# Weight sums of the gated half on the vector engine, and the place of the casts of loaded sums, in a gMLP layer

## The chip, the cores and the metric

The kernel runs on one core of a Trainium2 chip. Its engines work side by side, each through its own queue in order: TensorE (PE in the profile; PEld is its weight load), VectorE (DVE), ScalarE (ACT), GpSimd (POOL) and SyncE (SP), which here only issues DMAs. The metric is the device time of one execution in microseconds (us); lower is better. Runs of before lie between 1413.17 and 1414.5 us.

## What is computed

Two layers of a residual trunk over 512 tokens of width 1024, all in float32. Each has a token mixer and a squared-ReLU MLP, both normed and modulated. Layer 0 mixes with chunked attention; layer 1 with a spatial gating, which is where the change lies:

```python
def chunked_spatial_gating(h, w_in, v_gain, w_s, b_s, w_out):
    z = jax.nn.gelu(h @ w_in, approximate=False)          # 512 x 6144
    u, v = jnp.split(z, 2, axis=-1)
    v = rms_norm(v, v_gain).reshape(B, nw, SG_WINDOW, SG_GROUPS, SG_HALF // SG_GROUPS)
...
    vm = jnp.einsum('gij,bnjgc->bnigc', w, v) + b_s.T...
    return (u * vm.reshape(B, S, SG_HALF)) @ w_out
```

`v`, the gated half, needs its norm over all 3072 columns before the first product with `u` can be made, so the kernel computes all of `v` first.

## The kernel before

**Products.** A float32 product is made of three passes: each operand is split into a high part, a cast to fp32r by ScalarE, and a low part, the rest, by VectorE (class `Split`, lines 485 and 486), and `mm3` runs high by high, high by low and low by high (line 92).

**Seven instead of eight.** A product of 512 x 1024 activations with a 1024 x 1024 piece of a weight is cut into 2 x 2 blocks and made with seven block products in place of eight (`seven`, line 611), a Strassen-like scheme. The seven right operands are sums of the weight's blocks: (0,0); (1,0); (0,0)+(0,1); (1,1); (0,0)+(0,1)+(1,1); (0,1)+(1,1); and the sum of all four. They are taken in the order m = 0, 1, 2, 4, 3, 5, 6. Each is handled in two halves (s = 0, 1), so a product is 14 steps of 12 matmuls. Block (0,0) is loaded as `x`, (1,0) as `z`, (1,1) as `y`, and with `near=True` block (0,1) as `w`.

How a sum comes about differs. `plus` (line 628) adds two SBUF tiles on VectorE. `grow` (line 625) has GpSimd issue a DMA that loads a block and adds it to the tile in SBUF. With `near`, m = 2 (x + w) and m = 3 (x + y) are made by `plus`; m = 5 (y grown by block (0,1)) and m = 6 (x grown by block (1,0)) by `grow`. A product so has 4 such loads. The tile of `w` is freed after m = 2 has used it, that of `z` after m = 1.

**The left operands** (sums of activation blocks) of the gating layer are made once, in its first such product, and kept (`Kept`).

**Steps.** A step has four parts: `load` (DMAs from SyncE's queue), `right` (sums and `Split` of the weight), `left`, and `mult` (the matmuls, and `put`, which reads PSUM). `Run(steps, 4, 3)` writes them down so that `right` stands three steps before its `mult` and `load` four before that. In the gating layer the order of the steps is: four steps of an ordinary product, p = 1 and p = 2 of the gated half (`Gate`, line 1417), then u0 (`Mix`, line 1545), the output product d0, u1, u2 and d1. What is written down is not yet the order of the queues: a planner with its own model of the times orders each engine's instructions at build time (the region after `any_order()`). `tc.issue_after(ins)` tells it that the instructions of a block have to stand behind `ins` on the engine of `ins`; it adds no wait.

**Putting.** `Gate.put` copies a first part out of PSUM (line 1430), adds the second (1433), takes the GELU (1434) and its squares (1436), and stores each finished pair of tiles to DRAM (`v_store`, line 1407, shown as vd<-s). `Mix.put` does the same for `u` (copy 1565, sum 1568, GELU 1569); `Mix.mix`, some steps later, scales the reloaded `v` (1577), splits it (cast 1581, rest 1582), multiplies it with the mixing matrix, joins it with `u` (1595) and turns the tile (1602, 1606).

**Slots.** All large tiles (512 KB) lie in 49 slots of SBUF. `Slots.get` takes the slot that was freed longest ago; whoever writes to it waits for its last user.

The MLPs use `seven` too, without `near`: there all sums are made by `grow`.

Of the kernel before, what the change touches and what calls it, by code (L numbers as in the profile page):

```python
# [12 lines left out]
AF = mybir.ActivationFunctionType  # L13
# [3 lines left out]
P = 128  # L17
# [8 lines left out]
SGH = 3072  # L26
# [26 lines left out]
def trunk_kernel(  # L53
# [20 lines left out]
    V, A, G, T, SP = nc.vector, nc.scalar, nc.gpsimd, nc.tensor, nc.sync  # L74
# [7 lines left out]
    SL = Slots(sp, NSLOT, "s")  # L82
    PS = Slots(pp, 8, "p")

    def f32(ap):
        return ap.bitcast(F32)

    def bank():
        return PS.get([P, 512], F32)
# [4 lines left out]
    def mm3(ps, lh, ll, rh, rl, start, stop, more=False):  # L94

        mm(ps, lh, rh, start, False, more)
        mm(ps, lh, rl, False, False, more)
        mm(ps, ll, rh, False, stop, more)
# [278 lines left out]
    loaded = [None]  # L377
# [113 lines left out]
    class Sum:  # L491
# [26 lines left out]
        def put(self, t, hf, ps, op=ALU.add, whole=True):  # L518
            if t not in self.y:
                self.y[t], self.ids[t] = SL.get([P, D], F32)  # L520
            dst = self.y[t][:, hf * 512:hf * 512 + 512]
            if (t, hf) in self.seen:
                V.tensor_tensor(dst, dst, ps, op)  # L523
            else:
                A.copy(dst, ps)
                self.seen.add((t, hf))
# [81 lines left out]
    def nothing():  # L608
        pass

    def seven(left, src, y, near=False):


        raw, op, ps = {}, {}, {}

        def block(i, j, s_):
            r0 = i * 512 + s_ * 256
            return src[r0:r0 + 256, j * 512:j * 512 + 512].rearrange("(k p) n -> p k n", p=P)

        def load(name, i, j, s_):  # L620
            raw[name, s_] = t, n = SL.get([P, 2, 512], F32)
            SP.dma_start(t, block(i, j, s_))

        def grow(i, j, name, s_):
            G.dma_start(raw[name, s_][0], block(i, j, s_), accum_op=ALU.add)  # L625

        def plus(a, b, s_):
            V.tensor_tensor(raw[a, s_][0], raw[a, s_][0], raw[b, s_][0], ALU.add)

        def right(m, name, add, s_):  # L630

            if near and m == 2:
                plus("x", "w", s_)
                SL.free(raw["w", s_][1])
            op[m, s_] = Split(raw[name, s_][0], [P, 2, 512])
            if near and m == 4:
                plus("x", "y", s_)
            if add is None:
                SL.free(raw[name, s_][1])
            elif not near or m > 2:  # L640
                grow(*add, name, s_)

        def mult(m, acc, first, outs, done, s_):
            a, b = left.op[m], op.pop((m, s_))
            for u in range(2):
                if first and s_ == 0:
                    ps[acc, u] = bank()
                p, pi = ps[acc, u]
                c = slice(u * P, u * P + P)
                for k in range(2):  # L650
                    kk = 2 * s_ + k
                    ah, al, bh, bl = a.hi[:, kk, c], a.lo[:, kk, c], b.hi[:, k, :], b.lo[:, k, :]
                    mm3(p, ah, al, bh, bl, first and kk == 0, kk == 3, not first)
                if s_:
                    for i, j, o, whole in outs:
                        y.put(2 * i + u, j, p, o, whole)
                    if done:
                        PS.free(pi)
            b.free()
            if s_:  # L660
                left.done(m)

        def prep(m, s_):
            if s_ == 0:
                left.prep(m)

        add, sub = ALU.add, ALU.subtract
        plan = (
            (0, ("x", 0, 0), ("x", (0, 1)), ("z", True, ((0, 0, add, False),), False)),
            (1, ("z", 1, 0), ("z", None), ("y", True, ((0, 0, add, False),), True)),  # L670
            (2, None, ("x", (1, 1)), ("v", True, ((1, 1, add, False),), False)),
            (4, ("y", 1, 1), ("y", (0, 1)), ("v", False, ((0, 1, add, False),), True)),
            (3, None, ("x", (1, 0)), ("z", False, ((0, 1, sub, False),), False)),
            (5, None, ("y", None), ("z", False, ((1, 1, sub, False),), False)),
            (6, None, ("x", None), ("z", False, ((1, 0, add, True),), True)),
        )

        def loads(m, b, s_):
            if near and m == 2:
                load("w", 0, 1, s_)  # L680
            if b:
                load(*b, s_)

        return [
            Step(
                lambda m=m, b=b, s_=s_: loads(m, b, s_),
                lambda m=m, r=r, s_=s_: right(m, *r, s_),
                lambda m=m, s_=s_: prep(m, s_),
                lambda m=m, p=p, s_=s_: mult(m, *p, s_),
            )  # L690
            for m, b, r, p in plan for s_ in range(2)
        ]
# [432 lines left out]
    for t in range(NT):  # L1125
        ps, pi = bank()
# [252 lines left out]
    for t in range(NT):  # L1379
        ps, pi = out_ps[t]  # L1380
# [4 lines left out]
    for t in range(NT):  # L1385
        ps, pi = bank()
# [13 lines left out]
    kept = Kept(lambda: norm.blocks)  # L1400
# [98 lines left out]

    steps = gate_steps(1)  # L1500
    for p in (1, 2):
        steps += seven(kept, b_w_in[0][:, SGH + p * 1024:SGH + (p + 1) * 1024], Gate(p), True)

    wsT = []
    bsT = cp.tile([P, SGG], F32, name="bsT")
# [39 lines left out]
    class Mix:  # L1545
# [13 lines left out]
        def put(self, t, hf, ps, op, whole):  # L1559
            if (hf, t // 2) not in self.u:  # L1560
                self.u[hf, t // 2] = SL.get([P, 2, 512], F32)
            dst = self.u[hf, t // 2][0][:, t % 2, :]
            if not whole and (t, hf) not in self.seen:
                self.seen.add((t, hf))
                A.copy(dst, ps)  # L1565
                return
            if not whole:
                V.tensor_tensor(dst, dst, ps, op)
            A.activation(dst, ps if whole else dst, AF.Gelu)
            late = 5 if (self.p, hf, t // 2) == (0, 0, 0) else 2  # L1570
            later.append((now[0] + late, lambda: self.mix(t, hf, dst)))

        def mix(self, t, hf, u):
            cb = 2 * self.p + hf
            vh = tp.tile([P, 512], F32, tag="tt", name="vh")
            v, vi = self.v[hf, t // 2]
            V.scalar_tensor_tensor(
                vh, v[:, t % 2, :], vr[:, t:t + 1], self.g[:, hf * 512:hf * 512 + 512], ALU.mult, ALU.mult
            )
            vs, i = SL.get([P, 2, 512], F32R)  # L1580
            A.copy(vs[:, 0, :], vh)
            V.tensor_tensor(vs[:, 1, :], vh, f32(vs[:, 0, :]), ALU.subtract)
            ps, pi = bank()
            c0 = 0
            parts = []
            while c0 < 512:
                g = (cb * 512 + c0) // SGC
                c1 = min(512, (g + 1) * SGC - cb * 512)
                parts.append((g, c0, c1))
                c0 = c1  # L1590
            for g, c0, c1 in parts:
                ws = wsT[g // 4][0][:, :, (g % 4) * P:(g % 4 + 1) * P]
                mm3(ps[:, c0:c1], ws[:, 0, :], ws[:, 1, :], vs[:, 0, c0:c1], vs[:, 1, c0:c1], True, True)
            for g, c0, c1 in parts:
                mark[0] = V.scalar_tensor_tensor(
                    u[:, c0:c1], ps[:, c0:c1], bsT[:, g:g + 1], u[:, c0:c1], ALU.add, ALU.mult
                )
            PS.free(pi)
            SL.free(i)
            ps, pi = bank()  # L1600
            for f in range(4):
                T.transpose(ps[:, f * P:(f + 1) * P], u[:, f * P:(f + 1) * P], ident)  # L1602
            if t % 2 == 0:
                gated[self.p, t // 2, hf] = SL.get([P, 4, 256], F32)
            o = t % 2 * P
            A.copy(gated[self.p, t // 2, hf][0][:, :, o:o + P], ps.rearrange("p (f q) -> p f q", f=4))
            PS.free(pi)
            if t % 2:
                SL.free(vi, self.u[hf, t // 2][1])
                if (hf, t // 2) == (0, 1):  # L1610
                    SL.free(self.gi)

    def then(f, *gs):
        def both():
            f()
            for g in gs:
                g()

        return both

    y = Sum()
# [8 lines left out]

    def mix_steps(p):
        m = Mix(p)
        out = seven(kept, b_w_in[0][:, p * 1024:(p + 1) * 1024], m, True)
        out[0].right = then(out[0].right, m.gain, lambda: m.take(0, 0))
        for i, hf, b in ((6, 1, 0), (8, 1, 1), (10, 0, 1)):
            out[i].right = then(out[i].right, lambda hf=hf, b=b: m.take(hf, b))
        return out
# [159 lines left out]
```

## Time and profile before

| | |
|---|---|
| median of 3 runs | 1413.53 us (1413.17 to 1414.5) |
| the profiled execution | 1416.04 us |
| its span, from the first to the last instruction | 1414.3 us |
| mean granted TensorE clock | 0.988 |
| loads that add up, from in_b_w_in, on POOL's queue | 20, median 8.2 us from issue to landing |
| loads that add up, from in_ffn_w, on POOL's queue | 48, median 5.9 us |
| plain loads from in_b_w_in on SP's queue | 48, median 5.1 us |
| casts L485 on ScalarE | 308, mean 1050 ns |
| subtractions L486 on VectorE | 308, mean 1223 ns |

In the groups of the profile a line stands with its engine, what it writes and reads (`s` is any slot, `p` any PSUM bank), its count and its mean duration; "idle before" is the time in which its engine had nothing else to do, with what ended it. The gating layer's seven-products run from about 690 us to 985 us. A wait for several things is put down to the one that ended last in the profile.

### The profile page before, as it was taken

What the parts mean: (1) busy time and instruction counts of PE and PEld (TensorE: products, weight loads), DVE (VectorE), ACT (ScalarE), POOL (GpSimd) and SP (SyncE); (2) the same over time, 40 slices, a digit from 0 to 9 for tenths busy, and PEclk for the clock granted to TensorE, in tenths of its full rate; (3) what the DMA queues carried; (4) which work ended last, traced back from release to release, by engine and by line L of the source; (5) the groups of instructions that cost most, each with busy time, mean ns of one, the idle gap of its engine ahead of it and who ended that gap; (6) DMA issues with size and microseconds to landing.
All of it is one profiled execution on the core that took longest, in us unless ns stands there. A gap on an engine that the chain in (4) does not pass through costs nothing.

```text
span 1414.3 us, 18911 instructions
## 1 busy us (share of the span) xinstructions
PE 1378.7 (97%) x7130; PEld 1177.0 (83%) x7130; DVE 978.7 (69%) x1422; ACT 744.0 (53%) x1248; POOL 95.0 (7%) x106
## 2 busy tenths in 40 slices
PE   8999999899999999999999899999999999999998
PEld 7899888789888888888877788887888988888887
DVE  6888998766657668668675687678856356665772
ACT  6537667555455545536475554556435454554530
POOL 0000000001101102000101100010000010100100
PEclk8999999999999999999999999999999999999999
DMA  9656566564667766447658747665548366655541
GB/s 374 231 144 207 157 194 202 196 245 105 155 194 166 193 209 133 157 170 291 179 171 252 179 149 223 174 161 177 161 122 268 71 155 178 141 167 124 114 149 60
DMA packets 100427, 250.87 MB, mean 177 GB/s; under 512 B 8808, under 2 KB 10224, under 8 KB 100336
## 3 DMA queue, kind: packets, MB, share of 16 engines
q1 hardware_dynamic: 79536, 205.62, 43.6%
q0 software_dynamic: 19072, 37.75, 16.2%
q10 hardware_dynamic: 1728, 6.29, 1.1%
q8 instruction: 56, 0.92, 0.3%
q14 instruction: 35, 0.29, 0.1%
HBM read 226.57 MB, written 14.68 MB: 171 GB/s over the span
## 4 chain that ended last, share of the span: by engine, by line
PE 74%; issue 11%; DMA 7%; DVE 6%; ACT 2%; POOL 0%; SPq 0%; POOLq 0%; DVEq 0%; ACTq 0%
PE p L92 71%; DMA s<-in_b_w_in 2%; DMA vd<-s 1%; DMA s<-xsg 1%; DVE s L958 1%; PE p L1235 1%; DVE s L486 1%; DVE s L1197 1%; DMA s<-s 1%; ACT s L485 1%; DVE s L1240 0%; PE p L1602 0%; DMA s<-in_ada_w 0%; PE p L315 0%; DMA s<-in_x 0%
## 5 line engine op out<-in xcount | busy, mean ns | idle before, releaser
L92 PE MATMUL p<-s,s 128*128 128x512 f32 (+2 forms) x6496 | 1317.1, 363 | 20.9 <-ACT s L1565 3.6
L92 PEld LDWEIGHTS p<-s,s 128*128 128x128 f32 x6496 | 1103.2, 190 | 208.3 <-DVE nm L1197 4.3
L486 DVE TENSOR_TENSOR s<-s,s 128x1024 fp32r<-128x1024 f32 x308 | 371.3, 1223 | 231.7 <-ACT s L485 181.0
L485 ACT CAST s<-s 128x1024 fp32r<-128x1024 f32 x308 | 316.6, 1050 | 227.4 <-PE p L92 101.5
L746 ACT ACTIVATE r<-p 128x512 f32<-128x512 f32 x64 | 38.2, 597 | 125.6 <-PE p L92 125.6
L194 DVE SCALAR_TENSOR_TENSOR s<-s,cs,s 128x1024 f32<-128x1024 f32 x70 | 89.7, 1281 | 12.2 <-DMA s<-in_ada_w 11.6
L625 POOL DMA_DIRECT2D s<-in_ffn_w x48 | 58.3, 1215 | 498.7 <-DVE s L486 395.1
L523 DVE TENSOR_TENSOR s<-s,p 128x512 f32<-128x512 f32 x76 | 50.4, 683 | 16.6 <-PE p L92 16.3
L388 ACT CAST s<-s 128x1024 fp32r<-128x1024 f32 x36 | 37.5, 1049 | 36.4 <-DMA s<-in_ffn_w 18.3
L389 DVE TENSOR_TENSOR s<-s,s 128x1024 fp32r<-128x1024 f32 x36 | 43.4, 1222 | 10.4 <-ACT s L388 10.1
L752 ACT ACTIVATE s<-r 128x256 f32<-128x256 f32 (+1 forms) x112 | 44.9, 442 | 1.4
L424 DVE TENSOR_TENSOR tr<-p,s 128x512 f32<-128x512 f32 (+1 forms) x33 | 22.0, 672 | 31.2 <-PE p L92 31.1
L536 DVE TENSOR_TENSOR s<-s,s 128x1024 f32<-128x1024 f32 x28 | 33.6, 1223 | 10.9 <-PE p L92 10.5
L625 POOL DMA_DIRECT2D s<-in_b_w_in x20 | 24.1, 1218 | 234.6 <-DVE s L486 165.1
L1202 ACT ACTIVATE s<-s,nm 128x128 f32<-128x128 f32 (+3 forms) x64 | 36.0, 564 | 7.0 <-DVE nm L1197 5.6
L319 ACT ACTIVATE tt<-p,mod,mod 128x128 f32<-128x128 f32 x64 | 24.0, 464 | 20.9 <-PE p L315 10.4
L304 ACT ACTIVATE s<-s 128x512 f32<-128x512 f32 x24 | 15.3, 638 | 34.8 <-DVE s L425 33.7
L425 DVE TENSOR_TENSOR s<-s,tr 128x512 f32<-128x512 f32 (+1 forms) x33 | 22.2, 674 | 15.4 <-DMA s<-xsg 14.7
L1240 DVE TENSOR_TENSOR s<-p,s 128x512 fp32r<-128x512 f32 (+3 forms) x64 | 29.3, 485 | 3.9 <-ACT s L1239 3.6
L1197 DVE CUSTOM_DVE_ANT_0 s<-p,s 128x128 f32<-128x128 f32 (+3 forms) x64 | 29.7, 486 | 2.8 <-PE p L92 2.7
L1239 ACT CAST s<-p 128x512 fp32r<-128x512 f32 (+3 forms) x64 | 25.1, 426 | 8.7 <-PE p L1235 7.6
L1235 PE MATMUL p<-ident,s 128*128 128x128 f32 x160 | 24.3, 274 | 3.1 <-ACT s L1202 1.5
(146 smaller groups left out, 770.6 us busy)
## 6 DMA issues: line engine op xcount, KB each, us to landing
s<-in_ffn_w SPq DMA_DIRECT2D x116, 512.0 KB, 4.3
s<-in_ada_w SPq DMA_DIRECT2D x96, 512.0 KB, 5.0
s<-in_ffn_w POOLq DMA_DIRECT2D x48, 512.0 KB, 5.9
s<-in_b_w_in SPq DMA_DIRECT2D x48, 512.0 KB, 5.1
s<-in_b_w_out SPq DMA_DIRECT2D x24, 512.0 KB, 4.4
s<-in_a_w_in SPq DMA_DIRECT2D x22, 512.0 KB, 4.6
s<-in_b_w_in POOLq DMA_DIRECT2D x20, 512.0 KB, 8.2
s<-s SPq DMA_DIRECT2D x64, 128.0 KB, 3.4
```

The source lines that it names most:

```text
L92: T.matmul(ps, lhsT, rhs, start=start, stop=stop, skip_group_check=more)
L194: V.scalar_tensor_tensor(acc, r, ck, acc, ALU.mult, ALU.add)
L388: A.copy(hi, raw)
L389: engs[len(ids) // 2 % len(engs)].tensor_tensor(lo, raw, f32(hi), ALU.subtract)
L485: A.copy(self.hi, raw)
L486: mark[0] = V.tensor_tensor(self.lo, raw, f32(self.hi), ALU.subtract)
L523: V.tensor_tensor(dst, dst, ps, op)
L625: G.dma_start(raw[name, s_][0], block(i, j, s_), accum_op=ALU.add)
L746: A.activation(r, ps, AF.Relu)
L752: A.activation(d, v, AF.Square)
L1197: V.tensor_tensor_reduce(out=pt[it], in0=ps[:, 0:n], in1=b["bias"][:, 512 - n:512], scale=-1.0, scalar=-NEG, op0=ALU.add, op1=ALU.min, acc ...
L1235: T.transpose(ps[:, it * P:(it + 1) * P], b["pt"][it][:, jt * P:(jt + 1) * P], ident)
```

## The change

`seven` no longer takes `near` but a tuple `own`, the numbers of the sums that VectorE makes. The two products of the gated half get all four, (2, 3, 5, 6): `w` is kept after m = 2, `y` is added to it and m = 5 reads `w`; `z` is kept after m = 1 and added to `x` for m = 6. The three products of `u` get (2, 3), which is what `near` was; the MLPs get none, as before.

Besides, `Mix` notes its newest GELU, copy out of PSUM, or cast of a scaled `v` in `waited`. While `right` of m = 3, 5 or 6 writes down a `Split` whose sum a load adds up, it does so behind that instruction on ScalarE's queue. In the products of `u` this holds for m = 5 and 6; in the second MLP for m = 3, 5 and 6; in the first MLP `waited` is still empty.

```diff
-    def seven(left, src, y, near=False):
+    waited = [None]
+
+    def seven(left, src, y, own=()):
...
+        def drop(name, s_):
+            SL.free(raw.pop((name, s_))[1])
+
         def right(m, name, add, s_):
 
-            if near and m == 2:
+            if m == 2 and 2 in own:
                 plus("x", "w", s_)
-                SL.free(raw["w", s_][1])
-            op[m, s_] = Split(raw[name, s_][0], [P, 2, 512])
-            if near and m == 4:
+                if 5 not in own:
+                    drop("w", s_)
+            if m == 5 and 5 in own:
+                name = "w"
+                plus("w", "y", s_)
+                drop("y", s_)
+            if m == 6 and 6 in own:
+                plus("x", "z", s_)
+                drop("z", s_)
+            loaded = m in (3, 5, 6) and m not in own
+            with tc.issue_after(waited[0].ins) if loaded and waited[0] is not None else nullcontext():
+                op[m, s_] = Split(raw[name, s_][0], [P, 2, 512])
+            if m == 4 and 3 in own:
                 plus("x", "y", s_)
             if add is None:
-                SL.free(raw[name, s_][1])
-            elif not near or m > 2:
+                if not (m == 1 and 6 in own):
+                    drop(name, s_)
+            elif {0: 2, 2: 3, 4: 5, 3: 6}[m] not in own:
                 grow(*add, name, s_)
...
-            if near and m == 2:
+            if m == 2 and 2 in own:
                 load("w", 0, 1, s_)
...
-        steps += seven(kept, b_w_in[0][:, SGH + p * 1024:SGH + (p + 1) * 1024], Gate(p), True)
+        steps += seven(kept, b_w_in[0][:, SGH + p * 1024:SGH + (p + 1) * 1024], Gate(p), (2, 3, 5, 6))
...
-                A.copy(dst, ps)
+                waited[0] = A.copy(dst, ps)
...
-            A.activation(dst, ps if whole else dst, AF.Gelu)
+            waited[0] = A.activation(dst, ps if whole else dst, AF.Gelu)
...
-            A.copy(vs[:, 0, :], vh)
+            waited[0] = A.copy(vs[:, 0, :], vh)
...
-        out = seven(kept, b_w_in[0][:, p * 1024:(p + 1) * 1024], m, True)
+        out = seven(kept, b_w_in[0][:, p * 1024:(p + 1) * 1024], m, (2, 3))
```

## The prediction

> **What bounds the kernel now.** I read the page first, for the span and the busy times.
>
> ```profile
> span 1414.3 us, 18911 instructions
> PE 1378.7 (97%) x7130; PEld 1177.0 (83%) x7130; DVE 978.7 (69%) x1422; ACT 744.0 (53%) x1248; POOL 95.0 (7%) x106
> ```
>
> TensorE is busy for 97% of the span, so only time in which it stands still, or runs at a lower clock, can be won. The windows by stage (columns: stretch, its length, busy us and count of each engine, granted clock, DMA share, GB/s) show how much of that lies in the gating layer, which is all that the change touches:
>
> ```profile
> 690.00:768.00 78.00, 73.75 (x311) 59.38 (x310) 52.61 (x53) 51.52 (x83) 9.67 (x8) 0.96 0.76 208
> 768.00:815.00 47.00, 42.55 (x190) 34.95 (x189) 32.64 (x50) 28.21 (x46) 4.81 (x4) 0.96 0.69 192
> 815.00:940.00 125.00, 125.00 (x618) 105.55 (x617) 94.32 (x124) 65.96 (x92) 4.82 (x4) 1.00 0.59 179
> 940.00:985.00 45.00, 41.60 (x190) 34.63 (x189) 35.20 (x46) 27.97 (x40) 4.83 (x4) 0.92 0.61 160
> ```
>
> 690 to 768 holds the two gated-half products p = 1 and 2, 768 to 815 most of the first mixing product u0, 940 to 985 the end of the third, u2. Between them (815 to 940) TensorE never stops. The list of waits, for PE alone between 690 and 1000, names what ended the stops:
>
> ```profile
> PE p L92 <- ACT s L1565: 3.6, 1, 3.6
> PE p L92 <- ACT s L1581: 3.4, 2, 2.7
> PE p L92 <- DVE s L486: 2.2, 1, 2.2
> PE p L92 <- ACT s L485: 1.8, 1, 1.8
> PE p L1602 <- DVE s L1595: 0.8, 1, 0.8
> ```
>
> That is five stops, 11.8 us. The timeline shows who stood behind whom (start, duration, engine, line; in brackets the idle time before and what ended it). I call them S1 (before 723.72), S2 (756.91), S3 (798.10), S4 (the 0.8 at L1602, near 813) and S5 (958.55, with a second part of 0.68 before 959.55).
>
> ```profile
> 715.87 3.90 ACT L485 CAST s<-s 128x1024 fp32r<-128x1024 f32 x4 [1.12 <-DMA s<-in_b_w_in]
> 721.31 2.35 DVE L486 TENSOR_TENSOR s<-s,s 128x1024 fp32r<-128x1024 f32 x2
> 723.72 31.39 PE L92 MATMUL p<-s,s 128*128 128x512 f32 x130 [2.24 <-DVE s L486]
> ...
> 755.81 1.04 ACT L485 CAST s<-s 128x1024 fp32r<-128x1024 f32 x1 [1.52 <-DMA vd<-s]
> 756.91 37.55 PE L92 MATMUL p<-s,s 128*128 128x512 f32 x156 [1.80 <-ACT s L485]
> ...
> 796.52 1.04 ACT L485 CAST s<-s 128x1024 fp32r<-128x1024 f32 x1 [3.25 <-DMA s<-in_b_w_in]
> 797.47 1.07 ACT L1565 COPY s<-p 128x512 f32<-128x512 f32 x2
> 798.10 14.70 PE L92 MATMUL p<-s,s 128*128 128x512 f32 x61 [3.64 <-ACT s L1565]
> ...
> 956.93 1.04 ACT L485 CAST s<-s 128x1024 fp32r<-128x1024 f32 x1 [3.65 <-DMA s<-in_b_w_in]
> 957.89 0.61 ACT L1581 CAST s<-vh 128x512 fp32r<-128x512 f32 x1
> 958.55 0.33 PE L92 MATMUL p<-s,s 128*128 128x128 f32 x1 [2.72 <-ACT s L1581]
> ```
>
> S3 is the plainest: ScalarE sat 3.25 us on a cast whose weights an accumulating load was still adding up, and the copies (L1565) that let TensorE go on with its PSUM bank stood behind that cast. S5 has the same form with the cast L1581 in the copies' place. In S1 the casts came late for the same reason and VectorE's subtractions after them; in S2 the last wait was for a store (vd) out of the slot that the cast was to fill.
>
> A stop costs more than itself, by the granted clock in three-microsecond windows (last but two column):
>
> ```profile
> 723.00:726.00 3.00, 2.28 (x6) 1.80 (x7) 3.00 (x4) 2.30 (x4) 0.00 (x0) 0.66 0.44 156
> 726.00:729.00 3.00, 3.00 (x12) 2.42 (x11) 2.27 (x3) 1.36 (x3) 0.00 (x0) 0.77 0.75 227
> ...
> 756.00:759.00 3.00, 2.03 (x6) 1.41 (x7) 1.23 (x1) 3.00 (x5) 0.25 (x1) 0.85 0.82 336
> 759.00:762.00 3.00, 3.00 (x9) 2.32 (x9) 2.57 (x3) 2.89 (x6) 0.96 (x1) 0.58 0.43 41
> ...
> 798.00:801.00 3.00, 2.90 (x9) 2.27 (x10) 2.48 (x5) 0.54 (x2) 0.00 (x0) 0.67 1.09 279
> 801.00:804.00 3.00, 3.00 (x12) 2.43 (x11) 1.40 (x2) 2.72 (x4) 0.12 (x1) 0.76 0.80 242
> ...
> 960.00:963.00 3.00, 3.00 (x12) 3.00 (x12) 2.92 (x5) 2.30 (x3) 0.00 (x0) 0.50 0.28 109
> 963.00:966.00 3.00, 3.00 (x9) 2.32 (x8) 3.00 (x5) 3.00 (x5) 0.00 (x0) 0.50 0.00 0
> ```
>
> Lost clock is 3 us times (1 - clock), summed: S1 1.02 + 0.69 = 1.7; S2 0.45 + 1.26 = 1.7; S3 0.99 + 0.72 = 1.7; S5 1.5 + 1.5 = 3.0. Whole prices: **S1 3.9, S2 3.5, S3 5.3, S4 0.8, S5 6.4, together 19.9 us.** That is the most the change can win.
>
> **Part 1: in p = 1 and 2, eight accumulating loads go and eight additions come.** The groups of lines L625 (690 to 770) and L628, windows, and a store from the chain that ended last give the terms:
>
> ```profile
> L625 POOL DMA_DIRECT2D s<-in_b_w_in x8: 1203/1203/1467, 695.9 to 758.8; - x8
>   ACT s L485: 16.8, 6
> DMA to landing us min/median/max: 6.3/8.8/9.7
> L628 DVE TENSOR_TENSOR s<-s,s x20: 1218/1222/1229, 668.5 to 940.7; 128x1024 f32<-128x1024 f32 x20
> 693.00:731.00 38.00, 35.61 (x149) 28.67 (x149) 30.05 (x30) 26.79 (x43) 4.85 (x4) 0.96 0.82 228
> 731.00:768.00 37.00, 35.14 (x147) 28.31 (x146) 20.73 (x20) 21.73 (x35) 4.82 (x4) 0.95 0.69 183
> 780.00:790.00 10.00, 10.00 (x46) 8.27 (x45) 6.15 (x6) 6.51 (x13) 2.41 (x2) 1.00 0.68 173
> 748.51 7.22 DMA vd<-s
> ```
>
> Removed: 8 issues on POOL's queue (1.2 us each, behind which only the next such issue stands: no price), and 16.8 us in which ScalarE's casts waited for their landing, six times. Nothing new is loaded: w (block 0,1) and z (block 1,0) are in SBUF already and are only kept. Added: 8 L628 additions of 1.22 us, 9.8 us of VectorE, 4.9 in each product. In p = 2 the cover is ample: 20.7 + 4.9 = 25.6 of 37 us. In p = 1 it is thin: 30.05 + 4.9 = 35.0 of 38 us, and the 38 hold S1's own 3.9, so of a stretch without S1 (34.1 us) nothing is left over. VectorE may begin earlier (the first L628 stands at 668.5, before p = 1), so I do not make it the limit for sure; but I take S1 as **traded**: the load's wait goes, VectorE's queue is late next, gain 0, between a loss of 0.9 (35.0 - 34.1) and a gain of 3.9. S2 I count as **gone**, 3.5 us. A step is 12 matmuls; at full clock 46 start in 10 us, so 2.6 us. Fourteen steps from 693, with S1, end p = 1 at about 733; the store of its last tile, for whose slot S2's cast waited, was issued at 748.51, because the waits for landings had put p = 2's first products ahead of p = 1's last. Without those waits it can go out some 15 us sooner, and VectorE has 11 us to spare there. Bounds: 3.5 gained, or a loss by the slots (below).
>
> **Part 2: slots.** The 49 slots go round in order. Walking through the code's gets and frees I count 14 to 19 free in p = 1 and 2, and some 105 gets in 28 steps, 3.75 a step. Holding two w and two z longer takes up to 4, so a slot comes round 4 gets, or 1.07 steps, sooner: 2.8 us less time for a slot's last user to end. What such users take:
>
> ```profile
> ACT s L485 <- DMA vd<-s: 9.1, 4, 2.8
> 791.90 9.30 DMA vd<-s
> ```
>
> I cost this at 0: about 14 gets are still 3.7 steps or 9.8 us, while a store takes 7.2 (the row above) to 9.3 us from its issue, and casts are asked for three steps ahead. Four casts wait for such stores already, 9.1 us in all, so this cover is not safe; it is the losing rival.
>
> **Part 3: the order of the casts in u0, u1, u2.** Two products of each (the sums that loads still add up), 4 casts each, 12 in all, may no longer stand ahead of the newest GELU or copy at the moment they are written down; that is, by the loop's three-step lead, behind the copies of two to three steps before, and for the last cast behind the GELUs of the fifth product. It is an order on ScalarE's own queue, no added wait. In S3 the copies go first: TensorE's last matmul before the stop ended at 798.10 - 3.64 = 794.46, so the first copy (half of 1.07, L1565) restarts it some 0.6 us later, not 3.64: gain 3.0 and the clock's 1.7, **4.7**. Behind the casts then stand the subtractions L486 of the same tiles and, three steps (7.8 us) later, their matmuls: cover enough unless VectorE is late. S4 (0.8) I leave. S5 is open both ways: its cast is of the moved kind, and L1581 could pass it (6.4 gained); but which vh cast the planner puts where is not ordered by the change, and those four loads remain. I take 0. The same marker lies on the casts of the last MLP, long after it: 0, at either end; the first MLP has none.
>
> **Sum.** S2 3.5 + S3 4.7 = 8.2 us. The profiled execution took 1416.04 us (1414.3 and 1.7 around it); 1416.04 - 8.2 = 1407.8. It lies 2.5 above the median 1413.53 of the runs, on which scale the forecast is **1405.3 us**.
>
> The price of S2 rests on a clock that falls after a stop of 1.80 us, as the 0.85 and 0.58 rows show. The Trainium skill, "TensorE: Matmul & The Clock Gate" (The HAM clock gate), lets the clock fall only after an idle window of about 3.4 us; by that S2 would give 1.8 and the sum would be 6.5 us, 1407.0. The trace disagrees: S1 and S2, both shorter, lost 1.7 us each.
>
> **Rivals.**
> *All the stops go*: S1 and S5 too. For: every one has a cast behind a load in its chain. 1413.5 - 19.9 + 0.6 = 1394.2; with S5 alone beside the forecast 1398.9. Against: VectorE's 35.0 us in p = 1, and loads in u2 that land late whatever stands first.
> *Traded*: the planner orders the whole layer anew, and new stops of S1's or S2's kind appear, from VectorE in p = 1 or from a moved cast that is now too late (the last cast of u0 has 7.8 us for GELU, cast and subtraction while VectorE is full). Two of 3.7 give 1405.3 + 7.4 = 1412.7: no change. For: this layer had five such stops; against: 815 to 940 runs the same code without one.
> *Slower, by slots*: casts in p = 1, p = 2 and u0 whose slot is a stored v tile wait 2.8 us longer. S2 stays and grows by 2.8, and two of the other waits on vd become stops of 2.8 + 1.7 each: 2.8 + 9.0 - 4.7 = +7.1, 1420.6. It decides once the planner asks for a cast a step before its turn: then 9.8 - 2.6 = 7.2 us is below a store's 7.2 to 9.3. Against: with p = 1's loads gone, its GELUs and stores come earlier.
>
> **How the numbers follow.** Forecast (1400 to 1410) 0.42, all stops 0.22, traded 0.21, slots 0.15. About 0.2% (2.8 us) can be told from no change, so same is 1410.7 to 1416.4. Faster: 0.42 + 0.22 + 0.03 of traded = 0.67; same 0.18; slower 0.15. For 8 in 10 I leave out the slots' 0.15 and 0.05 of the best: 1394 to 1416.
>
> **What would show it.** Right: 12 instead of 20 L625 loads from in_b_w_in and 28 instead of 20 L628; no stop before 760 with a vd store or a landing in front; in u0 the copies L1565 ahead of the cast that waits for its load, and clock 1.00 in the windows after. Wrong: VectorE over 95% busy in p = 1 with PE waiting for L486 or L628 there by more than S1; casts whose idle time ends on vd longer than 2.8 us; S3 in its old order. A total above 1416 would refute the forecast, and one below 1394 my holding back on S1 and S5.

## The result, and the profile after

The changed kernel takes **1404.98 us** (median; runs from 1402.75 to 1408.56), the kernel before 1413.53 us in the same comparison: ratio 0.9944, 95% interval 0.9921 to 0.9966. The forecast was 1405.3 us.

The profiled execution of the changed kernel took 1408.5 us, at the upper end of its runs. Its page:

```profile
span 1406.6 us, 18894 instructions
PE 1375.4 (98%) x7130; PEld 1175.7 (84%) x7130; DVE 986.5 (70%) x1430; ACT 744.0 (53%) x1248; POOL 85.4 (6%) x98
L630 DVE TENSOR_TENSOR s<-s,s 128x1024 f32<-128x1024 f32 x28 | 33.9, 1218 | 6.2 <-DMA s<-in_b_w_in 6.1
L627 POOL DMA_DIRECT2D s<-in_b_w_in x12 | 14.5, 1205 | 236.4 <-DVE s L486 231.9
```

Lines of `seven` lie 2 lower than before, those of `Gate` and `Mix` 16 lower. There are 28 additions (L630, before L628) where there were 20, and 12 adding loads (L627, before L625) where there were 20; ScalarE and TensorE do as much as before. The list of waits for PE between 680 and 1000 has three rows in place of five, but not smaller ones:

```profile
PE p L92 <- ACT s L485: 4.3, 1, 4.3
PE p L92 <- ACT s L1597: 3.3, 1, 3.3
PE p L92 <- DVE s L1584: 1.0, 1, 1.0
```

Windows by stage (p = 1, p = 2, u0) say where they are not:

```profile
693.60:730.50 36.90, 36.90 (x164) 30.54 (x165) 35.39 (x35) 29.38 (x43) 0.00 (x0) 1.00 0.52 173
730.50:767.00 36.50, 36.50 (x163) 30.23 (x162) 28.23 (x28) 24.42 (x43) 0.00 (x0) 1.00 0.56 190
767.00:814.00 47.00, 42.69 (x194) 35.49 (x193) 33.12 (x55) 27.62 (x44) 4.82 (x4) 0.93 0.65 173
```

In p = 1 and p = 2 TensorE never stops and its clock is 1.00: S1 and S2 are both gone. VectorE is busy for 35.4 of 36.9 us in p = 1, which is what the forecast had summed up (35.0), and TensorE does not wait for it. In u0 a stop remains. The timeline there:

```profile
780.29 0.33 ACTq L1423 DMA_DIRECT2D vd<-s  x1
789.62 1.04 ACT L485 CAST s<-s 128x1024 fp32r<-128x1024 f32 x1 [7.26 <-DMA vd<-s]
790.57 0.58 ACT L1581 COPY s<-p 128x512 f32<-128x512 f32 x1
790.72 11.49 PE L92 MATMUL p<-s,s 128*128 128x512 f32 x42 [4.31 <-ACT s L485]
```

S3 has not gone; it has another face. A cast waited 7.3 us for the store of a v tile to leave its slot, TensorE waited for that cast, and the copies (L1581, before L1565) stand behind it. The store went out at 780.29 (the first line) and took 9.2 us. The clock falls for longer than after S3, to 0.50 in two windows, though a part of that lies in the stop itself:

```profile
789.00:792.00 3.00, 1.28 (x3) 1.10 (x4) 1.30 (x2) 2.38 (x4) 0.00 (x0) 0.50 0.83 281
792.00:795.00 3.00, 3.00 (x8) 2.35 (x8) 2.39 (x4) 2.57 (x4) 1.20 (x1) 0.50 0.44 45
795.00:798.00 3.00, 3.00 (x13) 2.42 (x13) 2.42 (x4) 0.59 (x1) 0.00 (x0) 0.90 0.95 188
```

And S5 stands as it was, a cast that waits for its load with L1597 (before L1581) and TensorE behind it:

```profile
950.71 1.04 ACT L485 CAST s<-s 128x1024 fp32r<-128x1024 f32 x1 [4.16 <-DMA s<-in_b_w_in]
951.66 0.61 ACT L1597 CAST s<-vh 128x512 fp32r<-128x512 f32 x1
952.32 0.33 PE L92 MATMUL p<-s,s 128*128 128x128 f32 x1 [3.27 <-ACT s L1597]
```

To compare plans I add up TensorE's loss by stage over windows of 0.1 us (690 to 768, 768 to 830 and 930 to 990; PE does not stop between 830 and 930): time in which PE is not busy, plus the time in which it is busy times (1 - granted clock). Half speed that falls into a stop is counted once that way. Besides, the layer has a length of its own, from the transposes just ahead of p = 1 (L1516, 1532 after) to the first ones behind the layer (L207, for the last MLP). In the kernel before and in the changed one:

```profile
691.97 1.03 PE L1516 MATMUL p<-ident,s 128*128 128x128 f32 x8
1025.12 1.04 PE L207 MATMUL p<-ident,s 128*128 128x128 f32 x8
...
692.52 1.03 PE L1532 MATMUL p<-ident,s 128*128 128x128 f32 x8
1017.60 1.03 PE L207 MATMUL p<-ident,s 128*128 128x128 f32 x8
```

This is the table for the two kernels and all experiments below, one profiled execution each, beside the median of the runs:

| kernel | p = 1, 2: idle + clock | u0: idle + clock | u2: idle + clock | loss, us | layer, us | median, us | ratio to before (95% interval) |
|---|---|---|---|---|---|---|---|
| before | 4.3 + 3.4 | 4.5 + 1.7 | 3.4 + 3.4 | 20.6 | 333.2 | 1413.53 | 1 |
| the change | 0 | 4.3 + 2.4 | 4.3 + 2.9 | 13.9 | 325.1 | 1404.98 | 0.9944 (0.9921 to 0.9966) |
| sums only | 0 | 2.5 + 1.7 | 4.5 + 1.7 | 10.4 | 322.4 | 1404.54 | 0.9924 (0.9904 to 0.9943) |
| order only | 3.8 + 0 | 4.2 + 1.7 | 3.5 + 2.7 | 15.9 | 328.4 | 1413.98 | 0.9997 (0.9984 to 1.0011) |
| slots held only | 4.0 + 1.5 | 5.5 + 2.9 | 4.3 + 1.7 | 20.0 | 333.0 | 1414.88 | 1.0004 (0.9989 to 1.0019) |
| change, slots freed late | 0 | 4.0 + 1.7 | 6.2 + 3.0 | 14.9 | 326.4 | 1409.26 | 0.9962 (0.9948 to 0.9977) |
| sums only, additions doubled | 0 | 3.7 + 3.0 | 4.7 + 1.7 | 13.2 | 324.7 | 1406.47 | 0.9953 (0.9935 to 0.9970) |
| fifth sum only | 0.7 + 0 | 9.8 + 4.4 | 3.8 + 3.1 | 21.8 | 334.8 | 1415.57 | 1.0015 (1.0001 to 1.0029) |
| sixth sum only | 0.4 + 0 | 3.0 + 0 | 3.5 + 3.1 | 10.0 | 323.1 | 1403.20 | 0.9929 (0.9908 to 0.9949) |
| sums, u0 too | 0 | 1.5 + 0 | 3.4 + 3.1 | 8.0 | 319.9 | 1402.02 | 0.9906 (0.9889 to 0.9924) |
| sums, u2 too | 0 | 3.3 + 1.7 | 0.4 + 0 | 5.4 | 317.1 | 1397.93 | 0.9891 (0.9872 to 0.9910) |
| sums, u0 and u2 too | 0 | 1.5 + 0 | 0.4 + 0 | 1.9 | 313.7 | 1395.57 | 0.9877 (0.9856 to 0.9898) |
| the same, with the order | 0 | 1.5 + 0 | 0.6 + 0 | 2.1 | 314.5 | 1398.32 | 0.9889 (0.9870 to 0.9908) |
| sums, all five products | 0 | 1.5 + 0 | 0.9 + 0 | 2.3 | 314.5 | 1398.13 | 0.9883 (0.9867 to 0.9900) |

One of the six runs of sums only took 2334.94 us at a granted clock of 0.625; its ratio and the median given here leave it out.

From before to after the loss fell by 6.6 us, the layer by 8.1, the profiled executions by 7.5 (1416.04 - 1408.5) and the medians by 8.55. What is left of the layer when the loss is taken off is 311 to 313 us in all 14 traces, so the loss accounts for the layer's length within about 2 us. The program ahead of the layer, which no version changes, took 689.2 to 698.8 us in these traces; so two profiled executions may differ by more than the change is worth, for reasons that have nothing to do with it.

### The profile page after: what moved, and what is told of

Same layout as the page of the kernel before. It is cut to its first block, busy times and chain, and to the rows that moved or that the text cites. A ratio compares the mean times of both kernels' runs of the same rounds, so it can differ in the third digit from the quotient of the medians.

```text
span 1406.6 us, 18894 instructions
## 1 busy us (share of the span) xinstructions
PE 1375.4 (98%) x7130; PEld 1175.7 (84%) x7130; DVE 986.5 (70%) x1430; ACT 744.0 (53%) x1248; POOL 85.4 (6%) x98
## 2 busy tenths in 40 slices
DMA packets 98251, 246.68 MB, mean 175 GB/s; under 512 B 8680, under 2 KB 10096, under 8 KB 98160
## 3 DMA queue, kind: packets, MB, share of 16 engines
q0 software_dynamic: 16896, 33.56, 14.5%
## 4 chain that ended last, share of the span: by engine, by line
PE 78%; issue 9%; DVE 6%; DMA 4%; ACT 2%; SPq 1%; POOL 0%; DVEq 0%; POOLq 0%; ACTq 0%
PE p L92 76%; DMA s<-xsg 1%; DVE s L974 1%; DMA s<-in_a_w_in 1%; DMA vd<-s 1%; DVE s L1213 1%; DVE s L486 0%; SPq L1176 0%; PE p L1251 0%; DMA s<-in_ada_w 0%; PE p L1618 0%; ACT s L485 0%; DMA s<-in_ffn_w 0%; PE p L315 0%; DMA s<-in_x 0%
## 5 line engine op out<-in xcount | busy, mean ns | idle before, releaser
L627 POOL DMA_DIRECT2D s<-in_ffn_w x48 | 58.3, 1215 | 498.9 <-DVE s L486 395.6
L389 DVE TENSOR_TENSOR s<-s,s 128x1024 fp32r<-128x1024 f32 x36 | 43.4, 1222 | 10.6 <-ACT s L388 10.4
L536 DVE TENSOR_TENSOR s<-s,s 128x1024 f32<-128x1024 f32 x28 | 33.6, 1220 | 10.9 <-PE p L92 10.5
L630 DVE TENSOR_TENSOR s<-s,s 128x1024 f32<-128x1024 f32 x28 | 33.9, 1218 | 6.2 <-DMA s<-in_b_w_in 6.1
L319 ACT ACTIVATE tt<-p,mod,mod 128x128 f32<-128x128 f32 x64 | 24.0, 464 | 21.0 <-PE p L315 10.4
L425 DVE TENSOR_TENSOR s<-s,tr 128x512 f32<-128x512 f32 (+1 forms) x33 | 22.1, 673 | 15.2 <-DMA s<-xsg 14.5
L627 POOL DMA_DIRECT2D s<-in_b_w_in x12 | 14.5, 1205 | 236.4 <-DVE s L486 231.9
```

Of the source, the lines that this page charges most:

```text
L389: engs[len(ids) // 2 % len(engs)].tensor_tensor(lo, raw, f32(hi), ALU.subtract)
```

## The experiments

The theory that I took to the chip: the eight loads that go carry the gain, by S1 and S2 (7.4 us); the order carries none. Its rivals: the order carries it (S3, 4.7 us, as forecast), or the slots and VectorE give part of it back.

**Sums only.** The order of the casts is left out of the change.

```diff
-            loaded = m in (3, 5, 6) and m not in own
+            loaded = False
```

> The change without its second part: all four sums of p = 1 and 2 by VectorE, but no cast is put behind a GELU or copy. Theory A (the eight removed loads carry the gain): p = 1 and 2 run without a stop, S1 and S2 are gone, 3.9 + 3.5 = 7.4 us, and u0 has a stop of S3's form, a copy L1581 (1565 of before) behind a cast that waits for its load; about 1406 us. Theory B (the order of the casts carries the gain): 1411 to 1414 us. If the copies stand in front anyhow and the wait for a vd store in u0 is the same as with the whole change, the second part did nothing in u0 and the time is that of the whole change within 2 us, 1403 to 1407.

Measured 1404.54 us, ratio 0.9924 (0.9904 to 0.9943): the whole gain. p = 1 and 2 run without a stop, and u0 has one of S3's form, as theory A said:

```profile
790.29 1.05 ACT L485 CAST s<-s 128x1024 fp32r<-128x1024 f32 x1 [3.15 <-DMA s<-in_b_w_in]
791.25 0.58 ACT L1581 COPY s<-p 128x512 f32<-128x512 f32 x1
791.88 2.53 PE L92 MATMUL p<-s,s 128*128 128x512 f32 x6 [2.44 <-ACT s L1581]
```

**Order only.** The two gated-half products stay as before.

```diff
-        steps += seven(..., Gate(p), (2, 3, 5, 6))
+        steps += seven(..., Gate(p), (2, 3))
```

> The change without its first part: p = 1 and 2 keep their eight adding loads, and only the casts of the fifth and sixth sums of u0, u1, u2 are put behind the newest GELU or copy. Theory A: S1 and S2 stay as they were, with both clock drops (7.4 us), S3 goes (up to 5 us): 1408 to 1411 us. Theory B: 1405 us or less. If S3 only turns into a wait for a vd store, as in the whole change, no gain: 1413 us.

Measured 1413.98 us, ratio 0.9997 (0.9984 to 1.0011): no gain. Neither theory had the reason. No copy stands behind a waiting cast any more, but the casts of the scaled v (L1597) do, and TensorE waits for those:

```profile
804.72 1.99 ACT L485 CAST s<-s 128x1024 fp32r<-128x1024 f32 x2 [5.67 <-DMA s<-in_b_w_in]
806.62 0.61 ACT L1597 CAST s<-vh 128x512 fp32r<-128x512 f32 x1
808.75 0.38 PE L92 MATMUL p<-s,s 128*128 128x256 f32 x1 [3.83 <-ACT s L1597]
```

ScalarE waited longer for a load here (5.67 us) than in S3 (3.25); the order only chose who stood behind. Its profiled execution lost 4.7 us less than that of before, 3.4 of it because its two stops in p = 1 and 2 happened to cost no clock (the last section says how); the median shows no such gain.

**Slots held only.** The kernel before, with w and z freed as late as in the change.

```diff
-                SL.free(raw["w", s_][1])
+                if not hold:
+                    SL.free(raw["w", s_][1])
...
-                SL.free(raw[name, s_][1])
+                if not (hold and m == 1):
+                    SL.free(raw[name, s_][1])
+                if hold and m == 5:
+                    SL.free(raw["w", s_][1])
+                if hold and m == 6:
+                    SL.free(raw["z", s_][1])
```

> The kernel before, with its loads and its order, but w and z of p = 1 and 2 stay in their slots as long as in the changed kernel. Slot theory: casts that wait for vd stores wait longer (9.1 us on ScalarE before), S2 grows: 1414 to 1421 us. Rival: the slots have no price by themselves: within 2 us of 1413.5 us.

Measured 1414.88 us, ratio 1.0004 (0.9989 to 1.0019): the slots have no price that can be measured. Of the slot theory's 1414 to 1421 us everything above 1416.5 falls.

**Slots freed late.** The whole change, with the slot of a stored v tile given back two stores later (the last two when the kept left operands are given up).

```diff
-        SL.free(i)
+        stored.append(i)
+        if len(stored) > 2:
+            SL.free(stored.popleft())
```

> The whole change, but the slot of a stored v tile goes back to the ring two stores later, so that a cast gets a slot whose store has long landed. Slot theory: the stop in u0 that the trace of the changed kernel shows (4.3 us before 790.7, on a cast that waited 7.3 us for a vd store, and 3.4 us of clock) goes, 7.7 us, about 1397 us. Rival: the cast would have to wait for something else there, its load or VectorE, and at most 2 us are won: 1403 to 1405 us; or two slots fewer cost more than that elsewhere: over 1405 us.

Measured 1409.26 us, ratio 0.9962 (0.9948 to 0.9977): no better than the change, and by time its last rival (over 1405 us) came true. The wait for the store did go; ScalarE's waits (casts, between 690 and 1000) are

```profile
ACT s L485 <- DMA s<-in_b_w_in: 29.2, 10, 5.8
ACT s L485 <- DMA vd<-s: 2.5, 1, 2.5
```

where the change had 7.5 and 7.3. But the plan that came of it set casts ahead of their loads again, and TensorE stopped about as long in u0, for the join of v and u (L1615, before L1595), and longer in u2, for the sum of u (L1588, before L1568):

```profile
PE p L92 <- DVE s L1588: 6.2, 1, 6.2
PE p L1622 <- DVE s L1615: 4.0, 1, 4.0
```

So the store was what the cast waited for, but not why u0 has a stop. The suspicion moved to the adding loads that u0 and u2 still have.

**u0, u2, both, and all.** Sums only, and VectorE makes all four sums in more products (the condition is `p == 0`, `p == 2`, `p != 1`, or none).

```diff
-        out = seven(kept, ..., m, (2, 3))
+        out = seven(kept, ..., m, (2, 3, 5, 6) if p != 1 else (2, 3))
```

> Sums only (no order of casts), and u0 as well makes all four sums by VectorE: its four adding loads go, 4.9 us of VectorE come, two w and two z stay in slots. Load theory: the stop in u0 (2.4 us on the copies behind a cast, 1.7 us of clock, in the run with sums only) goes, about 4 us: 1401 us against 1405. Rival: VectorE, nearly full in u0 beside the mixing, takes the loads' place and a stop of at least that size remains: 1404 to 1409 us.

> Sums only, and u2 as well makes all four sums by VectorE; u0 and u1 keep their loads. Load theory: the stops near 950 and 962 (4.5 us on casts L1597 behind a cast that waits for a load, 1.7 us of clock) go: about 1399 us against 1405. Rival: the stop in u2 comes from VectorE or from the late output weights and not from those four loads: 1404 to 1407 us.

> Sums only, and u0 and u2 make all four sums by VectorE; only u1 keeps its four loads. Load theory: both remaining stops go, 10 us: about 1395 us. Rival: VectorE becomes the bound there: 1404 us or more.

> Sums only, in all five products of the layer: no load adds up on a weight of the layer any more. Load theory: as with u0 and u2, and u1, which has no stop, stays as it is: about 1395 us. Rival: u1 lies beside the output product d0 and has the fewest free slots (down to 3), so slots or VectorE open a stop there: 1398 to 1405 us.

Measured 1402.02, 1397.93, 1395.57 and 1398.13 us: the load theory holds the first three times. For all five the median lies at the edge of the rival's range (1398 to 1405), but no stop opened in u1; u1, which had none, brings nothing. In each stage the long stops went where its loads went and stayed where they stayed: u0 lost 1.5 us in the four plans without its loads and 3.0 us or more in the ten with them, u2 0.4 to 0.9 and 6.0 or more. With u0 and u2 done, the list of PE's waits is down to 1.8 us:

```profile
PE p L1618 <- ACT s L1622: 1.1, 1, 1.1
PE p L92 <- ACT s L485: 0.3, 1, 0.3
PE p L92 <- DVE s L486: 0.2, 1, 0.2
PE p L92 <- DVE s L1584: 0.2, 1, 0.2
```

This version beats both kernels: ratio 0.9877 (0.9856 to 0.9898), against 0.9944 for the change. VectorE is fuller in it and in nobody's way: in u0 54.4 us of 63, against 46.3 in the same stretch of the change (767 to 830; the layer begins 6.2 us later in this execution):

```profile
773.20:836.20 63.00, 61.52 (x305) 51.62 (x304) 54.44 (x82) 39.59 (x61) 0.00 (x0) 1.00 0.49 159
```

The traces also show how the loads reach a cast that waits for a store. The last v store, issued early in u0, took 5.9 to 9.3 us from issue to landing in the ten plans in which u0 has adding loads, at least one of which was under way beside it; in the four plans without them it took 2.9 to 3.3 us. First that store in the change, then in the version with u0 and u2:

```profile
L1423 ACTq DMA_DIRECT2D vd<-s x1: 326/326/326, 780.3 to 780.3; - x1
DMA to landing us min/median/max: 9.2/9.2/9.2
...
L1423 ACTq DMA_DIRECT2D vd<-s x1: 327/327/327, 786.7 to 786.7; - x1
DMA to landing us min/median/max: 3.2/3.2/3.2
```

So the stop that the change has in u0 hangs, by all that these traces show, on the adding loads too, by way of the store; how a load holds up a store is not shown.

**The same, with the order.** The whole change, u0 and u2 too.

> The version with all sums by VectorE in p = 1, p = 2, u0 and u2, with the order of the casts kept (it then binds only u1 and the second MLP). If the order is worth nothing: 1395 us as without it, within 2 us. If it brings the wait for a vd store back: 1399 us or more.

Measured 1398.32 us, 0.9889 (0.9870 to 0.9908), inside the interval of the run without the order, though 2.75 us above its median, not within 2; ScalarE's casts wait for no vd store. No gain can be seen in the order.

**Additions doubled.** Sums only, with a second pass over each of the eight new sums.

```diff
+        def same(a, s_):
+            t = raw[a, s_][0]
+            V.tensor_tensor(t, t, t, ALU.max)
...
                 plus("w", "y", s_)
+                same("w", s_)
...
                 plus("x", "z", s_)
+                same("x", s_)
```

> Sums only, with the eight new additions' cost doubled: after each a second pass over the same tile (the larger of the tile and itself) of 1.22 us. p = 1 then asks 40.3 us of VectorE in some 37 us. The forecast's theory (VectorE is next in p = 1, thin cover): stops in p = 1 of 3 us or more with a clock drop, 1409 us or more against 1405. Rival (VectorE works ahead of p = 1 and behind it, the cover is wide): under 2 us lost, no stop before 760: 1403 to 1407 us.

Measured 1406.47 us, 0.9953 (0.9935 to 0.9970), 1.9 us above sums only, with intervals that overlap. The windows of p = 1 and p = 2, at the same distance from the layer's start as those of the change above:

```profile
691.87:728.77 36.90, 36.90 (x164) 30.55 (x165) 35.05 (x35) 26.76 (x41) 0.00 (x0) 1.00 0.52 173
728.77:765.27 36.50, 36.50 (x163) 30.24 (x162) 34.76 (x34) 26.75 (x44) 0.00 (x0) 1.00 0.51 176
```

VectorE is busy for 95% of both, and TensorE does not stop once. In p = 1 the doubling did not even make it busier (35.1 us, 35.4 in the change); in p = 2 it did (34.8, 28.2 in the change). So the work for a product does not lie in its own stage alone. In the change itself four additions stand well ahead of p = 1, before 681 us, where the kernel before has two (668.54 and 672.01):

```profile
669.09 1.22 DVE L630 TENSOR_TENSOR s<-s,s 128x1024 f32<-128x1024 f32 x1
672.56 2.35 DVE L630 TENSOR_TENSOR s<-s,s 128x1024 f32<-128x1024 f32 x2
679.28 1.22 DVE L630 TENSOR_TENSOR s<-s,s 128x1024 f32<-128x1024 f32 x1 [3.17 <-DMA s<-in_b_w_in]
```

**One sum at a time.** Sums only, with (2, 3, 5) and with (2, 3, 6) for p = 1 and 2.

> Sums only, but in p = 1 and 2 VectorE makes m = 2, 3, 5; the sixth is still made by four adding loads, and only w is kept longer. If the fifth sum's loads made the stops: 1405 us. If the sixth's did: 1413 us. If each made one of S1 and S2: about 1409 us.

> Sums only, but in p = 1 and 2 VectorE makes m = 2, 3, 6; the fifth is still made by four adding loads, and only z is kept longer. S1 stood at the fifth product, whose cast had waited 5.9 us: if the fifth sum's loads made the stops, about 1413 us; if the sixth's did, 1405 us; if each made one, 1409 us.

Measured 1415.57 us (1.0015; 1.0001 to 1.0029) and 1403.20 us (0.9929; 0.9908 to 0.9949). By the totals the sixth sum's loads would be the whole matter, but the table says otherwise: p = 1 and 2 are nearly free of stops in both (0.7 and 0.4 us). Half of the loads gone is enough there. The difference lies in u0, which has the same code in both: with the fifth sum only, the plan set a cast 7.85 us ahead of its load, with the copies behind it:

```profile
787.49 1.04 ACT L485 CAST s<-s 128x1024 fp32r<-128x1024 f32 x1 [7.85 <-DMA s<-in_b_w_in]
792.39 0.57 ACT L1581 COPY s<-p 128x512 f32<-128x512 f32 x1
793.01 2.50 PE L92 MATMUL p<-s,s 128*128 128x512 f32 x5 [6.65 <-ACT s L1581]
```

Why the planner did so in the one and not in the other stays open.

One thing no run separates: without the adding loads 4.2 MB less is moved (246.68 MB after, 250.87 before). Whether p = 1 and 2 would also run through with the eight blocks loaded plainly a second time and added by VectorE was not tried.

## Why the prediction was right or wrong

The total, 1405.3 against 1404.98, came out by two errors of opposite sign.

- *S2 gone, 3.5 us*: right, and p = 1 and 2 run through in every run that has all four sums there. Of the reason given a part is right: the store in question, the eighth of v, went out at 743.1 in place of 748.5, 5 to 6 us sooner and not 15, and it landed in 2.6 us in place of 7.2, which the forecast had not counted on.
- *S1 traded, gain 0*: wrong; it went, 3.9 us. The step that failed is "VectorE's queue is late next". The sum behind it was right in size (35.0 us forecast, 35.4 measured), and in part by luck, since the planner did some of p = 1's additions ahead of the stage and some of p = 2's in it. Its meaning was not right: with the cost doubled VectorE was busy for 95% of p = 1 and p = 2 and still no stop came. A share of busy time is no wait as long as the engine may work ahead.
- *S3 gone, 4.7 us, by the order of the casts*: wrong. "The copies go first" is what the order does, but in u0 TensorE then waited for what stood behind the cast next, a cast of scaled v (order only, 3.83 us) or a cast in a slot not yet stored (the change, 4.31 us). What had to go was the load, as the runs with u0's sums showed.
- *S4 left, S5 open and taken as 0*: S4 is not in PE's list after; S5 stayed (6.8 us before, 7.2 after by the table), as taken. Its price of 6.4 us was 0.4 too small, because the two rows of the clock leave out the ends of the fall. It went with u2's loads.
- *Slots, cost 0*: right by the time (slots held only). The mechanism of the losing rival did appear in the change, as the 7.26 us wait for a vd store in u0, one of the forecast's own signs of being wrong (longer than 2.8 us). Its price was not additional, since a stop stood at that place in nearly every plan, and the store was slow beside adding loads (9.2 us).
- *Traded*, new stops under a new plan: a stop in u0 of 2.4 to 6.7 us appeared in some form in every plan in which u0 kept its loads and p = 1 and 2 had lost all or half of theirs, except with the sixth sum only, where it was split into pieces of 0.3 to 1.5. So this rival was partly true, and it is why 4.7 us of the forecast did not come.

By the table p = 1 and 2 gave 7.6 us (S1 and S2) where 3.5 were forecast, and u0 and u2 took back 0.6 and 0.4 where 4.7 were forecast as a gain: 6.6 together. The layer became 8.1 us shorter and the medians differ by 8.55, against 8.2 forecast. The 1.5 us between loss and layer lie within the 2 us or so that the loss leaves open. So the agreement to 0.3 us is luck in good part.

## What to carry to other kernels

Where several engines' work is planned ahead, take the unpredictable wait away, not one of its victims. The adding loads landed 6.3 to 9.7 us after their issue in p = 1 and 2; they held up whatever came to stand behind them, and the stores beside them too, and an order by hand only picked the next victim here. Eight more VectorE additions of 1.22 us, on an engine that was 96% busy in its stage, were cheaper than eight loads that cost their issuing engine next to nothing (GpSimd, 9.7 of 78 us). Read a change's worth stage by stage (idle time, and lost clock of the rest), since a plan made anew shifts stops between stages and a right total can hide two wrong terms.

## What the runs showed of the hardware

The clock's fee is not in proportion to the stop. It comes in pieces of 3.41 us at half clock, about 1.7 us each. In the kernel before they begin at 723.95, 758.08, 799.04 and 959.47 us (there two in a row): 10, 12 and 47 times 3.413 us apart, so all lie on one grid. What counts is how a stop lies to that grid. S2's 1.80 us lay within one step and was followed by a piece at half clock; in the run with the order only a stop of 2.29 us at about the same place was cut in two by a step's end (1.27 and 1.08 us of idle time in the two steps) and paid none. Three steps of each, first of the kernel before:

```profile
754.67:758.08 3.41, 1.61 (x6) 0.68 (x5) 1.19 (x1) 2.27 (x4) 0.00 (x0) 1.00 1.03 416
758.08:761.49 3.41, 3.35 (x9) 2.65 (x9) 2.09 (x3) 3.41 (x7) 1.21 (x1) 0.50 0.37 62
761.49:764.90 3.41, 3.41 (x17) 2.80 (x16) 2.66 (x3) 0.40 (x1) 0.00 (x0) 1.00 1.00 217
...
751.37:754.78 3.41, 2.14 (x10) 1.45 (x8) 1.23 (x1) 2.78 (x5) 0.00 (x0) 1.00 1.06 336
754.78:758.19 3.41, 2.33 (x9) 1.62 (x10) 1.23 (x1) 3.41 (x6) 0.54 (x1) 1.00 0.79 320
758.19:761.60 3.41, 3.41 (x17) 2.80 (x16) 3.27 (x3) 2.60 (x6) 0.67 (x1) 1.00 0.61 64
```

In the 14 traces, from 600 to 1380 us, half clock always began on such a grid. A step at full clock with 1.8 us of idle time or more was followed by half clock in all 20 cases, one with 1.25 us or less in none; of the 12 between (1.26 to 1.79 us), 3 were. So equal stops may differ by 1.7 us, which may be part of the spread of the runs. The Trainium skill, "TensorE: Matmul & The Clock Gate" (What's actually happening), has the gate watch a free-running window of about 3.4 us; the grid agrees with that. Its rule that the clock falls after an idle window of about 3.4 us does not fit the 1.80 us of S2.

Adding loads that are issued close together land one behind the other. The four of u2 in the kernel before were issued between 941.35 and 946.14 us and landed 6.2, 9.6, 12.8 and 14.5 us after their issue; ScalarE's casts start as they land, at 947.60, 952.23, 956.93 and 960.70, and S5 stands behind the third. A view of these four loads sums it up:

```profile
DMA to landing us min/median/max: 6.2/11.2/14.5
```
